# A gated linear recurrence's chunk levels, with decay products carried upward in place of per-level exponentials of log sums

## The chip, the cores and the metric

The kernel runs on one core of a Trainium2 chip. The metric is the device time of one execution in microseconds (us). Three runs of the kernel before took 2473.97, 2474.93 and 2476.08 us; their median is 2474.93 us.

## What is computed

Two layers of a decoder trunk, for 512 tokens of width 1024. Each layer normalises, projects to four token mixers (A to D) and four gates, merges the branches, and goes on with a cross-attention and a gated MLP. Only mixer C, HGRN2, is touched. Its recurrence is this, with q, log_f, k and i from the projection, four heads of 64 keys and 64 values:

```
def step(state, xs):
    qc, lfc, kc, ic = xs                       # one chunk
    b = jnp.cumsum(lfc, axis=2)
    o_inter = jnp.einsum('bhck,bhkv->bhcv', qc * jnp.exp(b), state)
    diff = b[:, :, :, None, :] - b[:, :, None, :, :]
    decay = jnp.exp(jnp.where(causal, diff, -jnp.inf))
    att = jnp.einsum('bhtk,bhtsk,bhsk->bhts', qc, decay, kc)
    o = o_inter + jnp.einsum('bhts,bhsv->bhtv', att, ic)
    b_last = b[:, :, -1:, :]
    state = (jnp.exp(b_last[:, :, 0, :])[..., None] * state
             + jnp.einsum('bhsk,bhsv->bhkv', kc * jnp.exp(b_last - b), ic))
    return state, o
```

The pair (t, s) of att needs the decay between s and t, a product over f = exp(log_f). The kernel works in chunks of 128 tokens and takes this apart by levels: at level h, blocks of 2h tokens are halved, the later half of q carries the decay from the block's middle up to t, the earlier half of k the decay from s up to the middle, and one matmul gives all pairs between the two halves. Levels h = 1, 2, 4, ..., 64, and a level 0 for the diagonal, fill the whole triangle.

## The kernel before

**Dense work.** Every projection is done as three fp32r matmuls for one (mm3, L494): high parts by high, high by low, low by high. Weights come in chunks: a DMA on SyncE, ACT's cast of the high part (whi, L483), DVE's subtraction for the low part (wlo, L484). A tile of 512 columns takes 24 such matmuls into a PSUM buffer pd.

**Order.** The class Weave (L295) interleaves dense tiles with the latency-bound chains of the branches. It keeps a modelled time of TensorE (L282); a chain that yields v comes back no sooner than about 0.86 v us of this time later, and dense work is issued meanwhile. Thus the yields in branch_c set how many dense matmuls lie between two pieces of it on TensorE. Each engine then works through its own instructions strictly in the order in which they stand.

**Around branch C.** In a layer the projection of C (Cp) comes first. Then the chain of branch C (Cb) runs between the matmuls of the projection of D (Dp) and of the gates (gb, gd, gc); the chain of branch D (Db) needs Dp and Cb; the projection of B (Bp) needs Db. Each tile of Dp leaves PSUM by DVE's L1008 (draw), then POOL subtracts the shifted tile (ddd, L1009), then DVE's L1012 makes dr, dk, dv and so on.

**branch_c.** L800 sums log_f by scans. level(h) makes one operand tile cX for a level: DVE subtracts the sum at the block's middle (L813), ACT takes the two exponentials (L814, L815), POOL multiplies one half by q (L816), the other by k (L817). Level 0 uses k and q themselves, level 1 a tile from first() (L823 to L825). The operands of a level are made one level ahead in the program. Then yield 3, and 16 matmuls (32 instructions in the trace) into four PSUM buffers of the pool ps, which has just four. Each buffer goes to the attention tile catt, by DVE under a mask (L857) or, from h = 32, by ACT (L854). Then come khat (L866 to L868), q times exp(b) (L870), the transposes of khat (L876) and the recurrence over four chunks, which ends in the tile cy (L925).

Of the kernel before, what the change touches and what calls it, by code (L numbers as in the profile page):

```python
# [13 lines left out]
AF = mybir.ActivationFunctionType  # L14
ALU = mybir.AluOpType
# [6 lines left out]
P = 128  # L22
KD = D // P
NT = S // P
# [236 lines left out]
def bc(ap, pos, n):  # L261

    shape = list(ap.shape)
    shape.insert(pos, n)
    return ap.unsqueeze(pos).to_broadcast(shape)
# [108 lines left out]
class Trunk:  # L374
    scale = 0.856
# [296 lines left out]
    def layer_consts(self, l):  # L672
# [13 lines left out]
        nc.vector.tensor_mul(t.rearrange("p (a c) -> p a c", a=2), lam[:, :, 0], lam[:, :, 1])  # L686
        nc.vector.tensor_reduce(dv[:, 8:10], t.rearrange("p (a c) -> p a c", a=2), axis=AX.X, op=ALU.add)
        nc.scalar.activation(dv[:, 8:10], dv[:, 8:10], AF.Exp)
# [101 lines left out]
    def branch_c(self, l, q, f, i, g):  # L790
        nc, ar = self.nc, self.ar
        k = ar.alloc([P, 2, 512], name='ck')
        lf = ar.alloc([P, 2, 512], name='clf')
        self.logsig(l, f, k, lf)
        yield 8
        b = f
        for j in range(2):
            for t in range(NT):
                s = slice(t * P, (t + 1) * P)
                nc.vector.tensor_tensor_scan(b[:, j, s], self.ones, lf[:, j, s], 0.0, op0=ALU.mult, op1=ALU.add)  # L800
        od = lambda x, o: x.rearrange("p j (n a) -> p j n a", a=2)[:, :, :, o]

        def flat(x):
            return x.rearrange("p j t -> p (j t)")

        def level(h):
            X = ar.alloc([P, 1024], name='cX')
            v = X.rearrange("p (n a) -> p n a", a=2 * h)
            bv = flat(b).rearrange("p (n a) -> p n a", a=2 * h)
            qv = flat(q).rearrange("p (n a) -> p n a", a=2 * h)  # L810
            kv = flat(k).rearrange("p (n a) -> p n a", a=2 * h)
            nseg = 1024 // (2 * h)
            nc.vector.tensor_sub(v, bv, bv[:, :, h - 1:h].to_broadcast([P, nseg, 2 * h]))  # L813
            nc.scalar.activation(v[:, :, h:], v[:, :, h:], AF.Exp)  # L814
            nc.scalar.activation(v[:, :, :h], v[:, :, :h], AF.Exp, scale=-1.0)  # L815
            nc.gpsimd.tensor_mul(v[:, :, h:], v[:, :, h:], qv[:, :, h:])  # L816
            nc.gpsimd.tensor_mul(v[:, :, :h], v[:, :, :h], kv[:, :, :h])  # L817
            return X.rearrange("p (j t) -> p j t", j=2), X

        def first():  # L820

            X = ar.alloc([P, 2, 512], name='cX')
            nc.scalar.activation(od(X, 1), od(lf, 1), AF.Exp)  # L823
            nc.gpsimd.tensor_mul(od(X, 1), od(X, 1), od(q, 1))
            nc.gpsimd.tensor_copy(od(X, 0), od(k, 0))  # L825
            ar.free(lf)
            return X, X


        mm = self.te.matmul  # L830
        att = [[ar.alloc([P, 4, P], name='catt') for u in range(2)] for p in range(2)]
        for a in att[0] + att[1]:
            nc.gpsimd.memset(a, 0.0)
        levels = [0, 1, 64, 32, 16, 8, 4, 2]
        nxt = ((k, q), None)
        for n, h2 in enumerate(levels):
            (lhs, rhs), Xt = nxt
            if n + 1 < len(levels):
                X, xt = level(levels[n + 1]) if n else first()
                nxt = ((X, X), xt)  # L840
            yield 3
            for u in range(2):

                ps = [self.pss().rearrange("p (n t) -> p n t", n=4) for _ in range(2)]
                for x in range(4):
                    j, o = x % 2, (2 * u + x // 2) * P
                    for p in range(2):
                        r = slice(p * 64, p * 64 + 64)
                        mm(ps[p][:, x], lhs[r, j, o:o + P], rhs[r, j, o:o + P], start=True, stop=True)
                for p in range(2):  # L850
                    a = att[p][u]
                    if h2 >= 32:
                        for c in range(0, P, 2 * h2):
                            nc.scalar.copy(a[c:c + h2, :, c + h2:c + 2 * h2],  # L854
                                           ps[p][c:c + h2, :, c + h2:c + 2 * h2])
                    else:
                        nc.vector.copy_predicated(a, bc(self.um_('U%d' % h2), 1, 4), ps[p])  # L857
            if Xt is not None:
                ar.free(Xt)

        bv = b.rearrange("p j (t a) -> p (j t) a", a=P)
        el = self.small([P, 8], 'cel', 1)
        nc.scalar.activation(el, bv[:, :, P - 1], AF.Exp)
        kh = ar.alloc([P, 2, 512], name='ckh')
        khv = kh.rearrange("p j (t a) -> p (j t) a", a=P)
        nc.vector.tensor_sub(khv, bv[:, :, P - 1:P].to_broadcast([P, 8, P]), bv)  # L866
        nc.scalar.activation(kh, kh, AF.Exp)
        nc.gpsimd.tensor_mul(kh, kh, k)  # L868
        nc.scalar.activation(b, b, AF.Exp)
        nc.vector.tensor_mul(q, q, b)  # L870
        ktm = k
        yield 6
        for j in range(2):
            ps = self.pss()
            for t in range(NT):
                self.te.transpose(ps[:, t * P:(t + 1) * P], kh[:, j, t * P:(t + 1) * P], self.c('ident'))  # L876
            nc.scalar.copy(ktm[:, j], ps)
        ar.free(kh)
        yield 2
        y = ar.alloc([P, NT, 256], name='cy')  # L880
        st = None
        for t in range(NT):
            o = t * P
            ps = self.pss()
            pv = ps[:, 0:256].rearrange("p (h v) -> p h v", h=4)
            for h in range(4):
                mm(pv[:, h], att[h % 2][t // 2][:, (t % 2) * 2 + h // 2], i[:, t, h * 64:h * 64 + 64],
                   start=h == 0, stop=t == 0 and h == 3)
            if t:
                for j in range(2):  # L890
                    mm(ps[:, j * P:(j + 1) * P], q[:, j, o:o + P], st[:, j], start=False, stop=j == 1)
            nc.scalar.copy(y[:, t], ps[:, 0:256])
            if t < NT - 1:
                p2 = self.pss()
                for h in range(4):
                    r0 = (h % 2) * 64
                    j = h // 2
                    mm(p2[r0:r0 + 64, j * 64:j * 64 + 64], ktm[:, j, o + r0:o + r0 + 64],
                       i[:, t, h * 64:h * 64 + 64], start=True, stop=True)

                new = self.cp.tile([P, 2, P], F32, tag='bd%d' % (t % 2), bufs=1, name=self.nm('cbd'))
                nc.gpsimd.memset(new, 0.0)
                for j in range(2):
                    for r0 in (0, 64):
                        r = slice(r0, r0 + 64)
                        if t == 0:
                            nc.vector.tensor_copy(new[r, j, r], p2[r, j * 64:j * 64 + 64])
                        else:
                            nc.vector.scalar_tensor_tensor(new[r, j, r], st[r, j, r],
                                                           el[r, j * 4 + t:j * 4 + t + 1],  # L910
                                                           p2[r, j * 64:j * 64 + 64], op0=ALU.mult, op1=ALU.add)
                st = new
                yield 1.5
        ar.free(att, f, i, q)
        sq = ktm
        yv = y.rearrange("p t (h v) -> p (t h) v", v=64)
        sqv = sq.rearrange("p j (n v) -> p (j n) v", v=64)
        nc.scalar.square(sqv, yv)
        ss = self.small([P, 16], 'css', 1)
        rs = self.small([P, 16], 'crs', 1)  # L920
        nc.vector.tensor_reduce(ss, sqv, axis=AX.X, op=ALU.add)
        nc.vector.tensor_scalar(ss, ss, 1.0 / 64, EPS, op0=ALU.mult, op1=ALU.add)
        self.rsqrt(rs, ss, 'r16')
        nc.gpsimd.tensor_mul(y, y, g)
        nc.vector.tensor_mul(yv, yv, bc(rs, 2, 64))  # L925
        ar.free(sq, g)
        yield 7
        out = self.to_fm(y, 2, lambda j: self.cv('hng', 0))
        ar.free(y)
        return out  # L930
# [1102 lines left out]
```

## Time and profile before

| | |
|---|---|
| median of three runs | 2474.93 us |
| the profiled execution | 2476.26 us |
| its span in the trace | 2474.5 us |
| mean granted TensorE clock | 0.990 |
| TensorE (PE) busy | 2405.6 us, 97% of the span |
| VectorE (DVE) / ScalarE (ACT) / GpSimd (POOL) busy | 62% / 40% / 20% |
| share of PE in the chain that ended last | 87% |

The busy line tells how much of the span an engine worked. The waits tell for each engine which instruction waited for which, and for how long. Windows give busy time and granted clock by stretch. The chain is the work that ended last, followed back from the end; a timeline lists one engine's instructions by start, with the idle time ahead of each and what ended it in brackets. The levels of branch C run in layer 0 at about 73 to 126 us, in layer 1 at about 1295 to 1350 us.

### The profile page before, as it was taken

Reading aid. Unit: us, or ns where it says so; the run is one execution under the profiler, and the core shown is the slowest. Engines: PE = TensorE matmul, PEld = TensorE weight load, DVE = VectorE, ACT = ScalarE, POOL = GpSimd, SP = SyncE. Lnnn points to the kernel's source line nnn. Section 1 sums busy time; section 2 is a strip of 40 time slices with the busy share of each in tenths; the row PEclk is TensorE's granted clock in tenths of the full one; section 3 lists DMA queues with packets and bytes.
Section 4 is the critical chain, followed back from the end, with each engine's and each line's share of the span. In section 5 each row is a group of like instructions: output and inputs, shape, how many; then the busy total and the mean of one; then the engine's idle time right before and its main releaser. Section 6 shows DMA issues by size and latency. Waiting matters only on the chain.

```text
span 2474.5 us, 34381 instructions
## 1 busy us (share of the span) xinstructions
PE 2405.6 (97%) x13344; PEld 2005.7 (81%) x13344; DVE 1528.1 (62%) x2731; ACT 991.9 (40%) x1759; POOL 504.7 (20%) x390
## 2 busy tenths in 40 slices
PE   8899999999999999999999999999999999999997
PEld 7777887788889888888887788877888898888886
DVE  7677356856655567367476764477566565763762
ACT  6343523444334444234362425244434354442441
POOL 2421033245010111011232200433430101110112
PEclk9999999999999999999999999999999999999998
DMA  5224334214434222222322342332243242322321
GB/s 175 84 88 157 94 115 145 73 61 146 130 106 142 77 90 98 97 99 94 133 75 71 107 150 85 120 120 73 71 160 111 98 145 68 95 93 94 102 94 60
DMA packets 89602, 259.69 MB, mean 105 GB/s; under 512 B 18144, under 2 KB 21856, under 8 KB 89440
## 3 DMA queue, kind: packets, MB, share of 16 engines
q1 hardware_dynamic: 57168, 205.81, 25.3%
q10 hardware_dynamic: 25872, 30.58, 3.8%
q0 software_dynamic: 6400, 21.11, 2.7%
q8 instruction: 105, 1.72, 0.3%
q14 instruction: 57, 0.47, 0.1%
HBM read 234.32 MB, written 23.13 MB: 104 GB/s over the span
## 4 chain that ended last, share of the span: by engine, by line
PE 87%; DVE 6%; POOL 2%; ACT 2%; issue 1%; DMA 1%; DVEq 0%; ACTq 0%; SPq 0%; POOLq 0%
PE ffn_pd L288 29%; PE A_pd L288 7%; PE Bp_pd L288 5%; PE mo_pd L288 4%; PE mq_pd L288 4%; PE mix_pd L288 4%; PE ga_pd L288 4%; PE gd_pd L288 4%; PE gc_pd L288 3%; PE Db_ps L288 3%; PE Dp_pd L288 2%; PE gb_pd L288 2%; PE mv_pd L288 2%; PE mk_pd L288 2%; PE matt_ps L288 2%; PE Cb_ps L288 2%
## 5 line engine op out<-in xcount | busy, mean ns | idle before, releaser
L483 ACT CAST whi<-wst 128x1024 fp32r<-128x1024 f32 x388 | 406.1, 1051 | 786.2 <-PE ffn_pd L288 216.1
L484 DVE TENSOR_TENSOR wlo<-wst,whi 128x1024 fp32r<-128x1024 f32 x388 | 494.4, 1278 | 213.1 <-ACT whi L483 211.9
L288 PE MATMUL ffn_pd<-xgh,whi 128*128 128x512 f32 x704 | 274.3, 390 | 0.0
L288 PE MATMUL ffn_pd<-xgh,wlo 128*128 128x512 f32 x704 | 273.9, 389 | 0.0
L288 PE MATMUL ffn_pd<-xgl,whi 128*128 128x512 f32 x704 | 273.9, 389 | 0.0
L1897 POOL TENSOR_TENSOR ffn_ft<-ffn_ft,ffn_fc 128x512 f32<-128x512 f32 x44 | 60.1, 1367 | 545.6 <-DVE ffn_fu L1883 350.3
L288 PEld LDWEIGHTS ffn_pd<-xgh,wlo 128*128 128x128 f32 x704 | 132.2, 188 | 27.7
L288 PEld LDWEIGHTS ffn_pd<-xgl,whi 128*128 128x128 f32 x704 | 132.2, 188 | 27.3
L288 PEld LDWEIGHTS ffn_pd<-xgh,whi 128*128 128x128 f32 x704 | 132.2, 188 | 27.1
L288 PE MATMUL ffn_pd<-fh,whi 128*128 128x512 f32 x352 | 136.9, 389 | 0.0
L288 PE MATMUL ffn_pd<-fl,whi 128*128 128x512 f32 x352 | 136.9, 389 | 0.0
L288 PE MATMUL ffn_pd<-fh,wlo 128*128 128x512 f32 x352 | 136.9, 389 | 0.0
L288 PE MATMUL A_pd<-xgh,whi 128*128 128x512 f32 x256 | 106.0, 414 | 0.0
L288 PE MATMUL A_pd<-xgh,wlo 128*128 128x512 f32 x256 | 101.2, 395 | 0.0
L288 PE MATMUL A_pd<-xgl,whi 128*128 128x512 f32 x256 | 100.8, 394 | 0.0
L1884 DVE TENSOR_TENSOR ffn_fu<-ffn_pd,r_rbc 128x512 f32<-128x512 f32 x88 | 60.4, 688 | 43.8 <-PE ffn_pd L288 43.6
L531 DVE TENSOR_TENSOR fl<-ffn_ft,fh 128x512 fp32r<-128x512 f32 x44 | 30.5, 693 | 90.5 <-ACT fh L530 90.5
L530 ACT CAST fh<-ffn_ft 128x512 fp32r<-128x512 f32 x44 | 27.3, 621 | 144.8 <-POOL ffn_ft L1897 144.8
L1446 POOL TENSOR_TENSOR A_rp<-A_rp,snr 128x512 f32<-128x512 f32 x24 | 50.7, 2113 | 165.4 <-DVE A_rp L1445 163.3
L575 POOL TENSOR_TENSOR mo_sqa<-mo_sqa,mo_sqt 128x512 f32<-128x512 f32 x14 | 23.6, 1685 | 297.7 <-ACT mo_sqa L571 257.7
L1886 ACT ACTIVATE ffn_fc<-ffn_fu,cvt 128x512 f32<-128x512 f32 x88 | 71.7, 817 | 26.9 <-DVE ffn_fu L1884 26.7
L288 PEld LDWEIGHTS ffn_pd<-fl,whi 128*128 128x128 f32 x352 | 66.1, 188 | 13.8
(593 smaller groups left out, 6240.6 us busy)
## 6 DMA issues: line engine op xcount, KB each, us to landing
wst<-in_wst_dram SPq DMA_DIRECT2D x388, 512.0 KB, 3.5
gb_gate<-gb_gu ACTq DMA_DIRECT2D x16, 256.0 KB, 2.2
gd_gate<-gd_gu ACTq DMA_DIRECT2D x16, 256.0 KB, 2.1
gc_gate<-gc_gu ACTq DMA_DIRECT2D x16, 256.0 KB, 2.0
pc_gu<-gc_gate POOLq DMA_DIRECT2D x16, 256.0 KB, 3.7
pd_gu<-gd_gate POOLq DMA_DIRECT2D x16, 256.0 KB, 3.2
pb_gu<-gb_gate POOLq DMA_DIRECT2D x16, 256.0 KB, 3.0
x<-in_x_dram ACTq DMA_DIRECT2D x13, 256.0 KB, 3.5
```

The costliest lines, as they stand in the source:

```text
L288: return self.te.matmul(out, lhsT, rhs, **kw)
L483: nc.scalar.copy(hi, st)
L484: nc.vector.tensor_sub(lo, st, hi.bitcast(F32))
L530: nc.scalar.copy(dst[0], src)
L531: nc.vector.tensor_sub(dst[1], src, dst[0].bitcast(F32))
L575: (eng or nc.gpsimd).tensor_add(acc[:, :n], acc[:, :n], t[:, :n])
L1446: nc.gpsimd.tensor_mul(t2, t2, self.snr)
L1884: nc.vector.tensor_mul(u[:, 2:514], ps, self.rb)
L1886: nc.scalar.activation(acc, u[:, 2:514], AF.Identity, scale=self.cv('cw2', ch), bias=self.cv('cb', ch))
L1897: nc.gpsimd.tensor_mul(th, th, cc[1])
```

## The change

The scans, level() and first() go. The decay d = exp(log_f) is taken once (by ACT, over all tokens). The levels run in the order 0, 1, 2, 4, ..., 64, and all matmuls take k and q themselves, which are changed in place between levels: after level 0, q is multiplied by f (DVE, 1024 elements a partition); after level h, the earlier half of k in each block is multiplied by the decay of the whole later half (POOL, L834) and the later half of q by that of the earlier half (DVE, L835), and d becomes the product of neighbouring pairs (L838), half as many as before. After level 64, k is khat and q is q times exp(b), and d the decay of the chunk, so the block behind the levels goes too. A level's yield is now 4.5 and stands behind it; the yield 6 ahead of the transposes has gone.

```diff
@@ -793,52 +793,23 @@
         lf = ar.alloc([P, 2, 512], name='clf')
         self.logsig(l, f, k, lf)
         yield 8
-        b = f
-        for j in range(2):
-            for t in range(NT):
-                s = slice(t * P, (t + 1) * P)
-                nc.vector.tensor_tensor_scan(b[:, j, s], self.ones, lf[:, j, s], 0.0, op0=ALU.mult, op1=ALU.add)
-        od = lambda x, o: x.rearrange("p j (n a) -> p j n a", a=2)[:, :, :, o]
-        def flat(x):
-            return x.rearrange("p j t -> p (j t)")
-        def level(h):
-            X = ar.alloc([P, 1024], name='cX')
-            v = X.rearrange("p (n a) -> p n a", a=2 * h)
-            bv = flat(b).rearrange("p (n a) -> p n a", a=2 * h)
-            qv = flat(q).rearrange("p (n a) -> p n a", a=2 * h)
-            kv = flat(k).rearrange("p (n a) -> p n a", a=2 * h)
-            nseg = 1024 // (2 * h)
-            nc.vector.tensor_sub(v, bv, bv[:, :, h - 1:h].to_broadcast([P, nseg, 2 * h]))
-            nc.scalar.activation(v[:, :, h:], v[:, :, h:], AF.Exp)
-            nc.scalar.activation(v[:, :, :h], v[:, :, :h], AF.Exp, scale=-1.0)
-            nc.gpsimd.tensor_mul(v[:, :, h:], v[:, :, h:], qv[:, :, h:])
-            nc.gpsimd.tensor_mul(v[:, :, :h], v[:, :, :h], kv[:, :, :h])
-            return X.rearrange("p (j t) -> p j t", j=2), X
-        def first():
-            X = ar.alloc([P, 2, 512], name='cX')
-            nc.scalar.activation(od(X, 1), od(lf, 1), AF.Exp)
-            nc.gpsimd.tensor_mul(od(X, 1), od(X, 1), od(q, 1))
-            nc.gpsimd.tensor_copy(od(X, 0), od(k, 0))
-            ar.free(lf)
-            return X, X
+        d = f
+        nc.scalar.activation(d, lf, AF.Exp)
+        ar.free(lf)
+        flat = lambda x: x.rearrange("p j t -> p (j t)")
+        d = flat(d)
+        dd = ar.alloc([P, 1024], name='cD')
+        nd = 0
         mm = self.te.matmul
         att = [[ar.alloc([P, 4, P], name='catt') for u in range(2)] for p in range(2)]
         for a in att[0] + att[1]:
             nc.gpsimd.memset(a, 0.0)
-        levels = [0, 1, 64, 32, 16, 8, 4, 2]
-        nxt = ((k, q), None)
-        for n, h2 in enumerate(levels):
-            (lhs, rhs), Xt = nxt
-            if n + 1 < len(levels):
-                X, xt = level(levels[n + 1]) if n else first()
-                nxt = ((X, X), xt)
-            yield 3
+        for h in (0, 1, 2, 4, 8, 16, 32, 64):
             for u in range(2):
                 ps = [self.pss().rearrange("p (n t) -> p n t", n=4) for _ in range(2)]
@@ -846,36 +817,34 @@
                     j, o = x % 2, (2 * u + x // 2) * P
                     for p in range(2):
                         r = slice(p * 64, p * 64 + 64)
-                        mm(ps[p][:, x], lhs[r, j, o:o + P], rhs[r, j, o:o + P], start=True, stop=True)
+                        mm(ps[p][:, x], k[r, j, o:o + P], q[r, j, o:o + P], start=True, stop=True)
                 for p in range(2):
                     a = att[p][u]
-                    if h2 >= 32:
-                        for c in range(0, P, 2 * h2):
-                            nc.scalar.copy(a[c:c + h2, :, c + h2:c + 2 * h2],
-                                           ps[p][c:c + h2, :, c + h2:c + 2 * h2])
+                    if h >= 32:
+                        for c in range(0, P, 2 * h):
+                            nc.scalar.copy(a[c:c + h, :, c + h:c + 2 * h], ps[p][c:c + h, :, c + h:c + 2 * h])
                     else:
-                        nc.vector.copy_predicated(a, bc(self.um_('U%d' % h2), 1, 4), ps[p])
-            if Xt is not None:
-                ar.free(Xt)
-        bv = b.rearrange("p j (t a) -> p (j t) a", a=P)
-        el = self.small([P, 8], 'cel', 1)
-        nc.scalar.activation(el, bv[:, :, P - 1], AF.Exp)
-        kh = ar.alloc([P, 2, 512], name='ckh')
-        khv = kh.rearrange("p j (t a) -> p (j t) a", a=P)
-        nc.vector.tensor_sub(khv, bv[:, :, P - 1:P].to_broadcast([P, 8, P]), bv)
-        nc.scalar.activation(kh, kh, AF.Exp)
-        nc.gpsimd.tensor_mul(kh, kh, k)
-        nc.scalar.activation(b, b, AF.Exp)
-        nc.vector.tensor_mul(q, q, b)
-        ktm = k
-        yield 6
+                        nc.vector.copy_predicated(a, bc(self.um_('U%d' % h), 1, 4), ps[p])
+            if not h:
+                nc.vector.tensor_mul(q, q, f)
+            else:
+                dv = d.rearrange("p (n a) -> p n a", a=2)
+                half = lambda x, o: flat(x).rearrange("p (n a) -> p n a", a=2 * h)[:, :, o * h:o * h + h]
+                to = lambda o: dv[:, :, o:o + 1].to_broadcast([P, 512 // h, h])
+                nc.gpsimd.tensor_tensor(half(k, 0), half(k, 0), to(1), op=ALU.mult)
+                nc.vector.tensor_tensor(half(q, 1), half(q, 1), to(0), op=ALU.mult)
+                d = dd[:, nd:nd + 512 // h]
+                nd += 512 // h
+                nc.vector.tensor_mul(d, dv[:, :, 0], dv[:, :, 1])
+            yield 4.5
+        el = d
+        ktm = ar.alloc([P, 2, 512], name='ckt')
         for j in range(2):
             ps = self.pss()
             for t in range(NT):
-                self.te.transpose(ps[:, t * P:(t + 1) * P], kh[:, j, t * P:(t + 1) * P], self.c('ident'))
+                self.te.transpose(ps[:, t * P:(t + 1) * P], k[:, j, t * P:(t + 1) * P], self.c('ident'))
             nc.scalar.copy(ktm[:, j], ps)
-        ar.free(kh)
+        ar.free(k)
         yield 2
         y = ar.alloc([P, NT, 256], name='cy')
         st = None
@@ -911,7 +880,7 @@
                                                            p2[r, j * 64:j * 64 + 64], op0=ALU.mult, op1=ALU.add)
                 st = new
                 yield 1.5
-        ar.free(att, f, i, q)
+        ar.free(att, f, i, q, dd)
         sq = ktm
         yv = y.rearrange("p t (h v) -> p (t h) v", v=64)
         sqv = sq.rearrange("p j (n v) -> p (j n) v", v=64)
```

Where instructions stand now. On POOL in layer 0, before, from the first work on branch C to the first ddd of Dp:

```order
L824 ISA
L824 TENSOR_TENSOR cX_673<-cX_673,cq_172 128x512
L825 COPY cX_673<-ck_602 128x512
L816 TENSOR_TENSOR cX_729<-cX_729,cq_172 128x8x64
L817 TENSOR_TENSOR cX_729<-cX_729,ck_602 128x8x64
...
L816 TENSOR_TENSOR cX_997<-cX_997,cq_172 128x256x2
L817 TENSOR_TENSOR cX_997<-cX_997,ck_602 128x256x2
L1009 TENSOR_TENSOR Dp_ddd_633<-Dp_draw_632 128x512
L1009 TENSOR_TENSOR Dp_ddd_690<-Dp_draw_689 128x512
```

And the same stretch of POOL in the changed kernel, where L978 is ddd and L834 the mul of k:

```order
L978 ISA
L978 TENSOR_TENSOR Dp_ddd_633<-Dp_draw_632 128x512
L978 TENSOR_TENSOR Dp_ddd_705<-Dp_draw_704 128x512
L834 TENSOR_TENSOR ck_602<-ck_602,cf_173 128x512
L978 TENSOR_TENSOR Dp_ddd_769<-Dp_draw_768 128x512
L834 TENSOR_TENSOR ck_602<-ck_602,cD_658 128x256x2
L978 TENSOR_TENSOR Dp_ddd_833<-Dp_draw_832 128x512
L834 TENSOR_TENSOR ck_602<-ck_602,cD_658 128x128x4
```

The cX operations ahead of ddd have gone, and the muls of k stand one by one between the ddd of the tiles.

On DVE in layer 0, before, the last rows ahead of the first copies into catt (L1008 is draw, L1012 the operation that needs ddd; rk and csr belong to a rotary table):

```order
L1008 TENSOR_TENSOR Dp_draw_632<-Dp_pd_592,r_rbc_291 128x512
L1007 MEMSET Dp_draw_689 128x1
L484 TENSOR_TENSOR wlo_897<-wst_894,whi_896 128x1024
L1012 SCALAR_TENSOR_TENSOR dr_587<-Dp_ddd_633,cvt_75,Dp_draw_632 128x512
L658 TENSOR_TENSOR rk_1241<-rk_1241 128x512
L659 TENSOR_SCALAR csr_1237<-rk_1241 128x512
L1008 TENSOR_TENSOR Dp_draw_689<-Dp_pd_638,r_rbc_291 128x512
L1007 MEMSET Dp_draw_786 128x1
L484 TENSOR_TENSOR wlo_964<-wst_961,whi_963 128x1024
L1012 SCALAR_TENSOR_TENSOR dr_587<-Dp_ddd_690,cvt_75,Dp_draw_689 128x512
L857 COPY_PREDICATED catt_665<-um,Cb_ps_705 128x512
L857 COPY_PREDICATED catt_667<-um,Cb_ps_706 128x512
```

In the changed kernel, DVE in layer 0 from level 4 to level 8 (L977 is draw, L981 the twin of L1012, L827 the copy, L835 the mul of q):

```order
L981 SCALAR_TENSOR_TENSOR dk_588<-Dp_ddd_833,cvt_75,Dp_draw_832 128x512
L827 COPY_PREDICATED catt_659<-um,Cb_ps_848 128x512
L827 COPY_PREDICATED catt_661<-um,Cb_ps_849 128x512
L827 COPY_PREDICATED catt_660<-um,Cb_ps_860 128x512
L827 COPY_PREDICATED catt_662<-um,Cb_ps_861 128x512
L835 TENSOR_TENSOR cq_172<-cq_172,cD_658 128x128x4
L977 TENSOR_TENSOR Dp_draw_923<-Dp_pd_838,r_rbc_291 128x512
L976 MEMSET Dp_draw_987 128x1
L484 TENSOR_TENSOR wlo_1130<-wst_1127,whi_1129 128x1024
L827 COPY_PREDICATED catt_659<-um,Cb_ps_896 128x512
L827 COPY_PREDICATED catt_661<-um,Cb_ps_897 128x512
L981 SCALAR_TENSOR_TENSOR dv_589<-Dp_ddd_924,cvt_75,Dp_draw_923 128x512
```

The subtractions of the levels have gone from DVE; each level now has its copies and then its mul of q, and the work of one tile of Dp stands around them.

On TensorE, in layer 0, before: 51 matmuls of Dp, level 0, then seven times 15 dense matmuls and a level, 27 dense ones and the transposes. Now: 36 of Dp, level 0, seven times 21 dense ones and a level, 21 and the transposes. Ahead of the matmuls of cy's transposes stand 30 matmuls of the gates in place of 38 in layer 0, 34 in place of 38 in layer 1; ahead of those of dsq in layer 0 43 in place of 46. Between the last operation of Db and Bp stand 23 in place of 43 (layer 0) and 7 in place of 24 (layer 1). From Bp on TensorE's order is the same, and no matmul is added or taken out.

## Rows read from the trace of the kernel before

**Rows 1.** The page: busy us, share of the span, instructions.

```profile
PE 2405.6 (97%) x13344; PEld 2005.7 (81%) x13344; DVE 1528.1 (62%) x2731; ACT 991.9 (40%) x1759; POOL 504.7 (20%) x390
```

**Rows 2.** Waits of PE: line, releaser: us in total, times, longest us.

```profile
PE Cb_ps L288 <- DVE catt L857: 14.5, 2, 8.8
PE Dp_pd L288 <- DVE wlo L484: 3.7, 1, 3.7
PE Db_ps L292 <- DVE dsq L1079: 3.3, 2, 2.0
...
PE Cb_ps L292 <- DVE cy L925: 2.6, 2, 2.1
```

**Rows 3.** Windows: us, busy PE PEld DVE ACT POOL, PEclk, DMA share, GB/s.

```profile
80.00:100.00 20.00, 12.32 (x89) 10.65 (x90) 15.63 (x22) 5.40 (x8) 6.93 (x5) 0.74 0.20 66
...
1280.00:1300.00 20.00, 16.29 (x84) 13.24 (x83) 20.00 (x13) 11.66 (x20) 20.00 (x11) 0.85 0.16 53
1300.00:1320.00 20.00, 14.35 (x96) 11.96 (x95) 13.36 (x19) 3.59 (x5) 8.75 (x6) 0.81 0.23 77
```

**Rows 4.** The chain of waits, layer 0: start us, us, what.

```profile
80.63 1.01 POOL Dp_ddd L1009
...
87.68 4.39 PE Cb_ps L288 x32
92.08 3.77 PE Dp_pd L288 x15
95.85 1.99 PE Cb_ps L288 x32
97.83 3.63 PE Dp_pd L288 x15
...
209.56 43.52 PE gd_pd L288 x192
```

**Rows 5.** POOL's timeline, both layers: start us, us, instruction, [idle before <- releaser].

```profile
46.95 1.73 POOL L824 TENSOR_TENSOR cX<-cX,cq 128x512 f32<-128x512 f32 x1 [15.50 <-ACT cX L823]
51.62 10.54 POOL L825 COPY cX<-ck 128x512 f32<-128x512 f32 x1 [2.93 <-ACT ck L774]
...
63.37 2.29 POOL L817 TENSOR_TENSOR cX<-cX,ck 128x512 f32<-128x512 f32 x1
...
74.00 1.26 POOL L817 TENSOR_TENSOR cX<-cX,ck 128x512 f32<-128x512 f32 x1
...
84.16 1.96 POOL L1009 TENSOR_TENSOR Dp_ddd<-Dp_draw 128x512 f32<-128x512 f32 x1 [2.53 <-DVE Dp_draw L1007]
...
97.66 2.40 POOL L868 TENSOR_TENSOR ckh<-ckh,ck 128x1024 f32<-128x1024 f32 x1
...
1274.57 0.88 POOL L825 COPY cX<-ck 128x512 f32<-128x512 f32 x1 [37.88 <-ACT ck L786]
```

**Rows 6.** DVE's timeline in the levels of layer 0.

```profile
81.66 0.75 DVE L1012 SCALAR_TENSOR_TENSOR dr<-Dp_ddd,cvt,Dp_draw 128x512 f32<-128x512 f32 x1 [11.25 <-POOL Dp_ddd L1009]
...
86.82 1.32 DVE L857 COPY_PREDICATED catt<-um,Cb_ps 128x512 f32<-128x512 uint8 x2
...
97.73 2.87 DVE L1012 SCALAR_TENSOR_TENSOR dk<-Dp_ddd,cvt,Dp_draw 128x512 f32<-128x512 f32 x1 [1.21 <-POOL Dp_ddd L1009]
...
101.66 0.68 DVE L1008 TENSOR_TENSOR Dp_draw<-Dp_pd,r_rbc 128x512 f32<-128x512 f32 x1
...
102.35 1.23 DVE L484 TENSOR_TENSOR wlo<-wst,whi 128x1024 fp32r<-128x1024 f32 x1
...
112.23 2.10 DVE L484 TENSOR_TENSOR wlo<-wst,whi 128x1024 fp32r<-128x1024 f32 x1 [0.16 <-ACT whi L483]
```

**Rows 7.** The chain of waits, layer 1.

```profile
1309.06 4.29 PE Cb_ps L288 x32
1313.35 4.06 PE Dp_pd L288 x15
```

**Rows 8.** PE's timeline, level 0 of layer 1.

```profile
1295.17 3.79 PE L288 MATMUL Cb_ps<-cq,ck 64*128 64x128 f32 x32
```

## The prediction

> **What bounds the kernel now.** The page's busy line comes first: TensorE (PE) works 97% of the span and no other engine comes near [rows 1]. An edit on another engine can then only pay where PE waits, or where the granted clock falls. The waits of PE, sorted by length, show where that is [rows 2]: the second largest entry is in the chunk levels of branch C (Cb_ps), 14.5 us in two waits, one per layer, released by the copies catt of L857. A wait of 3.7 us on wlo stands in layer 1 just ahead of its second one. The windows give the other half of the loss [rows 3]: the granted clock is 0.74, 0.85 and 0.81 of full speed in the 20 us around these waits.
>
> Two things are behind the wait. The chain shows POOL muls of L816 and L817 one behind the other until 80.63 us in layer 0, and only then L1009 (ddd), which DVE waits for, and behind DVE's L1012 the copies [rows 4]. The POOL timeline says why it is late: it has a copy and 13 muls to do in one row, each 1.26 us alone and up to 2.29 us, and the copy took 10.54 us [rows 5]. DVE works in order, so L1012 stood idle 11.25 us for ddd with the catt copies queued behind it [rows 6]. A level fills all four ps buffers, so the next level cannot begin before they are copied: PE waited 8.8 us. Layer 1 has the same row on POOL without the slow copy (0.88 us there), and its wait is 5.7 us (14.5 less 8.8).
>
> **What the loss is worth.** A level takes 1.99 us at full clock and the 15 dense matmuls between two levels 3.63 us [rows 4]. After the wait the level took 4.39 us, about twice: the granted clock was at 1.2 instead of 2.4 GHz. Layer 0 loses 8.8 + (4.39 - 1.99 = 2.4) + (3.77 - 3.63 = 0.1) = 11.3 us. Layer 1 loses 5.7 + 3.7 of waits, 3.79 - 1.99 = 1.8 on its level 0, 4.29 - 1.99 = 2.3 on the level after, 4.06 - 3.63 = 0.4 on the block after that [rows 7, 8], and 0.8 on the block that ran between (1309.06 less the 5.7 of wait less 1298.96, where level 0 ended, is 4.4 against 3.63), in all 14.7 us. Together **26.0 us**, about 1% of the time, and that is all there is to gain here unless other stages move.
>
> **The change part by part.** *What goes:* the log sums (scan, 6 subtractions), the exponentials per level and 14 of POOL's cX operations; khat's subtraction, exponential and mul. All this is off PE, and its worth is the 26.0 us if nothing new is late. In the new order POOL's first work is ddd, and DVE's L1012 twin no longer waits behind a row of muls. So the catt waits go. In layer 1 DVE and POOL are both busy in all of the 20 us ahead of the wait [rows 3], on the subtractions and muls, with wlo queued among them; these go too, so its 3.7 us goes.
>
> *What comes per level:* PE has the same 16 matmuls per branch level, and now 21 dense ones between levels instead of 15. A dense matmul is 43.52 / 192 = 0.227 us [rows 4]; 15 of them are 3.40 and the block took 3.63, so a switch adds 0.23. A block of 21 is 4.77 + 0.23 = 5.0, the period 1.99 + 5.0 = 7.0 us. DVE must do in a period: 7/8 of a dense tile (21 of 24 matmuls) and the level's own work. A tile costs it 0.68 (draw), 1.23 (wlo), 0.75 (L1012) and, where wlo lies beside ddd, 2.10 - 1.23 = 0.87 more [rows 6], 3.53 together, 7/8 of it 3.1. The level's own is four copies at 1.32 / 2 = 0.66, 2.64, and the half mul of q; as a 128x512 operation it is bounded by draw and L1012, I take 0.69. Sum **6.4 of 7.0 us**. DVE keeps up, with little to spare. The products d are tiny tiles and lie behind the q mul; they go with it.
>
> *Where it is tight:* the new order puts, at levels 4 and 8, a tile's end right at the level's start. From the level's start: draw to 0.7, ddd (1.01 to 1.96 [rows 4, 5]) to 2.7 at most, L1012's twin to 3.4, four copies to 6.1, q mul to 6.8, against a next level due at 7.0. In layer 1 another small DVE operation (dkk) stands in this row and uses the slack up. Also, POOL's k mul starts right behind ddd, so beside L1012's twin. The trace has this once: L1012 took 2.87 instead of 0.75 us beside the POOL mul L868 of 2.40 us [rows 5, 6]. The k mul is half as wide and takes 1.26 us, so I charge 1.3 less the slack. Low bound: no wait at all, 0. High bound: all four tight levels wait 1.3 and layer 1 half a us more for dkk, 4 x 1.3 + 2 x 0.5 = 6.2, with up to one clock fall of 2.4 in each layer, 11. The small waits that the trace shows (cy 2.1, dsq 2.0 [rows 2]) are the nearest; I take 1.5 us per layer, **3.0 us**.
>
> *The k mul on POOL:* 1.26 us (2.29 contended) from the level's end at 2.0 or ddd's at 2.7, done by 5.0 at the latest, due at 7.0. Costed at nothing; the cover is the block of 21 dense matmuls. If the cover were 15, 5.0 would still be inside 5.6.
>
> Whether DVE's copies suffer beside the k mul is the other open price. The trace has wlo, both inputs in SBUF, at 2.10 beside ddd and at 1.23 without; of a copy out of PSUM beside a POOL mul it has no clean case. The Trainium skill (GPSIMD Engine Reference, section 1, Specifications) has VectorE and GpSimd share SBUF interfaces, with contention for DVE instructions that have two SBUF inputs. By that rule, wlo, L1012 and the q mul suffer, the catt copies with one input in PSUM don't; the wlo rows agree as far as they go.
>
> *What moves behind the levels:* the transposes, cy, Db and gates shift against the dense work on PE: ahead of the transposes of Cb stand 21 matmuls instead of 27, ahead of cy's 30 instead of 38 in layer 0 and 34 instead of 38 in layer 1; after the last operation of Db, 23 instead of 43 and 7 instead of 24. From Bp on PE's order is the same. The waits there now are 2.6 (cy) and 3.3 us (dsq) in both layers [rows 2]. khat needs no work ahead of the transposes any more. Ahead of cy 4 to 8 matmuls less are 0.9 to 1.8 us more wait where there is one; dsq has 43 instead of 46 ahead in layer 0. Bounds -2 and +3; I take 0, since the earlier start of the whole chain offsets it.
>
> **Sum.** 26.0 - 3.0 = 23.0 us. The profiled execution took 2476.3 us (span 2474.5), 1.3 above the median of the runs, so 2476.3 - 23.0 = 2453.3 there and 2474.9 - 23.0 = **2452** for the median. With the bounds: waits 0 and cy -2 give 2447, waits of 11 and cy +3 give 2463; I narrow it to 2446 to 2458 for this case, since both ends need all terms to go one way.
>
> **Rivals.** *First: POOL's first mul pays a one-off.* The copy of 10.54 us in layer 0 against 0.88 in layer 1 [rows 5] is 9.7 us for something that occurs once. If it is a cost of POOL's first operations, it lands on the first ddd; some 4 us of it are covered, then PE waits 5.3 and the level after runs at half clock, 2.4: 2452 + 7.7 = 2460. Against it: the first mul L824 came ahead of the copy and took 1.73, and the new kernel has no POOL copy there. The Trainium skill (GPSIMD Engine Reference, section 2.1, Instruction dispatch) says that the first call of a freshly loaded kernel pays a load of about 6 us; by that figure the wait would be 1.6 us, 2452 + 1.6 + 2.4 = 2456, an estimate. The rows put it on another operation. 7%.
>
> *Second: DVE is the bound of each level.* If the copies too are slowed beside the k mul, by its 1.3 us in 6.4, DVE needs 7.7 of 7.0 us and PE waits 0.7 in each of five levels with DVE copies behind a k mul, plus the tight ones' 3: 5 x 0.7 x 2 layers = 7, 2452 + 7 = 2459. For it: 2.10 against 1.23 for wlo. Against: the copies' input in PSUM. 8%.
>
> *Third, slower:* the levels are now a serial chain. Before, the operands cX of all levels could be made ahead; now each level's k and q wait for the last matmul of the one before, and the next level for the mul. If the k mul with its broadcast operand takes far longer than a plain one, each of 14 gaps (7 per layer) waits. A wait of 1.5 us with the level at half clock costs 1.5 + 2.4 = 3.9, 14 times 55: 2475 - 26 + 55 = 2504. It decides from 26 / 14 = 1.9 us per gap, that is a k mul of over 7.0 + 1.9 - 2.7 = 6.2 us (4.3 before anything waits), with the clock kept; POOL's muls with strided operands in the trace are at 1.26 to 2.29 [rows 5]. 5%.
>
> *Fourth: no change.* The wait only moves, for instance to cy and Db, whose cover is thinner; 20 us would have to come back in stages with 6 us of waits now. 2475. 5%.
>
> **How the numbers follow.** The forecast has 75%. A run of this kernel tells a change from none from about 0.2%, 5 us. Faster: 75 + 7 + 8 = 90%; same 5%; slower 5%. The range from 2444 to 2461 leaves out the third and fourth rival and about 4% at each end of the first cases.
>
> **What would show it.** Right: no PE wait on the catt copies over 2 us, granted clock 1.00 in the levels of both layers, ddd the first POOL mul with about 1 to 2 us, L834 at 1.3 to 2.3, the copies still at 0.66, and waits of PE under 1.5 us at levels 8 and 16. Wrong: a first POOL operation of many us (first rival), copies near 1.3 (second), L834 over 4 us (third), waits on cy, dsq or Bp that have grown by 10 us or more (fourth).

## The result, and the profile after

The changed kernel takes 2490.11 us (median of 4 runs, 2486.84 to 2490.42) against 2474.45 us before (4 runs too): a ratio of 1.0059 with a 95% interval of 1.0042 to 1.0077. It is 0.6% **slower**; 2452 us, faster, was forecast, with a range that ended at 2461. The profiled execution took 2490.42 us, its span is 2488.6 us. One run among all that follow, of e5, took 10464 us in place of 2454 to 2455 and is left out.

The surprise is that what was forecast for the waits and the clock of the levels came true. These are the waits of PE after (line, releaser: us in total, times, longest):

```profile
PE Bb_ps L292 <- DVE bp L1497: 14.5, 13, 1.9
PE Cp_pd L288 <- ACT xgh L533: 9.8, 1, 9.8
PE Db_ps L292 <- DVE dsq L1048: 4.9, 2, 2.6
...
PE Cb_ps L292 <- DVE cy L894: 2.1, 2, 1.4
...
PE Cb_ps L288 <- DVE cq L835: 0.6, 1, 0.6
```

The 14.5 us on catt and the 3.7 us on wlo [rows 2] have gone; what the levels wait for now is 0.6 us for q. The windows of the stretches around the levels (us, busy PE, PEld, DVE, ACT, POOL, then the granted clock, DMA share, GB/s) have the clock at full speed, where it was at 0.74 and 0.81 [rows 3]:

```profile
80.00:100.00 20.00, 20.00 (x141) 16.03 (x143) 17.13 (x25) 4.55 (x5) 6.14 (x6) 1.00 0.23 77
...
1300.00:1320.00 20.00, 20.00 (x155) 16.19 (x155) 17.71 (x24) 3.15 (x3) 6.63 (x5) 1.00 0.17 54
```

So the time was lost elsewhere, and PE's busy time says what kind of loss it is. The page's busy line after:

```profile
PE 2439.0 (98%) x13344; PEld 1996.5 (80%) x13344; DVE 1513.4 (61%) x2729; ACT 973.4 (39%) x1728; POOL 455.6 (18%) x374
```

PE has the same 13344 instructions and is busy 33 us longer than in [rows 1], although less of them ran at half clock. The chain shows where. These are long pieces of undisturbed dense work and, of after, also a level and the block of 21 behind it (start us, us, what), first before, then after:

```profile
754.82 23.03 PE mk_pd L288 x192
...
884.53 348.19 PE ffn_pd L288 x1536
```

```profile
99.15 2.06 PE Cb_ps L288 x32
101.20 5.10 PE Dp_pd L288 x21
...
661.80 44.80 PE mix_pd L288 x192
...
753.18 22.72 PE mk_pd L288 x192
...
883.25 358.39 PE ffn_pd L288 x1536
```

1536 matmuls of the MLP, hundreds of us behind the change and with nothing to wait for, take 358.39 us in place of 348.19: 0.2333 us each against 0.2267, at a granted clock of 1.00 in both. The blocks of 256 columns that are shown (mk) became a little faster, 22.72 against 23.03. It is so in all of the dense work: from the start of one matmul of 512 columns to that of the next, the mean over some 7,700 steps is 0.2273 us before and 0.2331 us after, some 45 us in all, of which 1,890 steps of 256 columns (0.1204 and 0.1179 us) give 5 back. The two MLPs alone cost 20 us.

TensorE's instructions and their order there are the same in both kernels. What differs for them is where the tiles lie. The built programs place the pools one behind the other in each partition of SBUF: constants, weight buffers, small tiles, arena. The change takes out one small tile, cel (8 numbers, 32 bytes), and all of the arena moves down by 32 bytes:

```
first byte of               before    after
the weight buffers           33952    33952
the arena (activations)     113824   113792
difference, modulo 256           0      224
```

The experiments ask whether these 32 bytes are the cause.

### The profile page after: what moved, and what is told of

The parts are those of the page before. It is cut to its first block, busy times and chain, and to the rows that moved or that the text cites. A ratio compares the mean times of both kernels' runs of the same rounds, so it can differ in the third digit from the quotient of the medians.

```text
span 2488.6 us, 34307 instructions
## 1 busy us (share of the span) xinstructions
PE 2439.0 (98%) x13344; PEld 1996.5 (80%) x13344; DVE 1513.4 (61%) x2729; ACT 973.4 (39%) x1728; POOL 455.6 (18%) x374
## 3 DMA queue, kind: packets, MB, share of 16 engines
q8 instruction: 105, 1.72, 0.3%
## 4 chain that ended last, share of the span: by engine, by line
PE 92%; DVE 5%; ACT 1%; issue 1%; DMA 1%; POOL 0%; DVEq 0%; ACTq 0%; SPq 0%
PE ffn_pd L288 30%; PE A_pd L288 7%; PE Bp_pd L288 5%; PE gc_pd L288 4%; PE Cp_pd L288 4%; PE gd_pd L288 4%; PE mq_pd L288 4%; PE mo_pd L288 4%; PE mix_pd L288 4%; PE ga_pd L288 4%; PE Dp_pd L288 3%; PE Db_ps L288 3%; PE gb_pd L288 2%; PE matt_ps L288 2%; PE mk_pd L288 2%; PE mv_pd L288 2%
## 5 line engine op out<-in xcount | busy, mean ns | idle before, releaser
L288 PEld LDWEIGHTS ffn_pd<-fh,wlo 128*128 128x128 f32 x352 | 66.1, 188 | 16.1
```

Source lines behind the costliest of these rows:

```text
L288: return self.te.matmul(out, lhsT, rhs, **kw)
```

## The experiments

Theory P: dense matmuls are slower because the streamed activations now lie otherwise against the weights. Theory N: the new work or its order does it. Theory T: TensorE pauses less and therefore runs slower.

**e1, the tile back.** In branch_c of the changed kernel:

```diff
+        self.small([P, 8], 'pad', 1)
```

> The changed kernel with one unused tile of 32 bytes a partition put back into the pool of small tiles, where the small tile cel stood before. It moves the arena (all large tiles, so the activations that the dense matmuls stream) back by 32 bytes, to where it lay in the kernel before; instructions and their order stay. Theory P (placement): the dense 512-column matmul takes 0.2333 us in the changed kernel and 0.2267 before because the change took 32 bytes out ahead of the arena. Then a block of 192 goes back from 44.80 to 43.5 us and the time to 2452 us or a little under (2444 to 2456). Theory N (new program): the slowness comes with the new work or its order itself, and the time stays at 2490, a block of 192 at 44.8. Theory T (TensorE pauses less in the levels and so runs slower elsewhere): stays at 2490 too.

Measured: 2450.1 us, 0.990 of before (0.9884 to 0.9917). The same two blocks in its chain:

```profile
743.80 23.03 PE mk_pd L288 x192
873.48 348.22 PE ffn_pd L288 x1536
```

40 us come back by 32 unused bytes, with every instruction as it was. N and T fall. This kernel is also faster than both.

**e2, the same 32 bytes in the kernel before.**

```diff
+        self.small([P, 8], 'pad', 1)
```

> The kernel before with one unused tile of 32 bytes more among the small tiles, so that its arena starts a multiple of 64 bytes, as in the changed kernel, in place of 32 beyond one. Nothing else is changed. Theory P: a block of 192 dense matmuls takes 44.8 us in place of 43.5 and the time is 2515 us (2505 to 2525): 2474 and the some 40 us by which the changed kernel missed 2450. Theories N and T: 2474, as the program and its pauses are those of before.

Measured: 2517.1 us, 1.0169 (1.0153 to 1.0184), the MLP's block at 358.39. The old kernel becomes slower by 41 us with no change in its work.

**e3 and e4, the weights moved.** An unused tile among the constants moves the weights by 32 bytes; e4 has that and e1's.

```diff
+        self.cp.tile([P, 8], F32, name='pad')
```

> The changed kernel with an unused tile of 32 bytes among the constants, ahead of the weight buffers and the arena. Weights then start at a multiple of 64 bytes (they lay 32 beyond one in both kernels), the arena 32 beyond one, as before. If the place of the streamed activations alone decides: 2452 us, a block of 192 at 43.5. If it matters that weights and arena lie at a different offset: 2490, a block at 44.8, as they differ here and in the changed kernel, and agree in the kernel before. N and T: 2490.

> The changed kernel with both unused tiles, so that weights and arena start at multiples of 64 bytes. If the place of the streamed activations alone decides: 2490 us, a block of 192 at 44.8. If it matters that they differ: 2452, a block at 43.5, since they agree here. N and T: 2490.

Measured: e3 2489.5 us with the block at 358.39, e4 2449.4 us with 348.23. With these, e1 and e2, two places of the weights (33952 and 33984) have met the same two places of the arena (113824 and 113856): a difference of 0 modulo 256 is fast, 32 more or less slow, and neither place alone decides.

**e5, e10, e11, e13, e14: other differences.** The pad of e1 was made larger, to 24 numbers in e5, and to 40, 264, 72 and 136 in e10, e11, e13 and e14. Each differs from e1 by nothing but the arena's place (and that of the small tiles behind the pad).

```diff
-        self.small([P, 8], 'pad', 1)
+        self.small([P, 24], 'pad', 1)
```

> The changed kernel with an unused tile of 96 bytes among the small tiles in place of 32. Weights lie 32 beyond a multiple of 64 and of 128 bytes as ever; the arena now lies 32 beyond a multiple of 64, but 96 beyond one of 128. If the two have to agree to 64 bytes: a block of 192 dense matmuls at 43.5 us and 2450 us as with 32 bytes. If they have to agree to 128 bytes: 44.8 and 2490.

> The changed kernel with an unused tile of 160 bytes: arena and weights lie at the same offset to 128 bytes, as in the kernel before, but differ by 128 to 256. With 96 bytes (agreement to 64, not to 128) a block of 1536 dense 512-column matmuls took 351.6 us against 348.2 and one of 192 256-column matmuls 21.8 against 23.0. If agreement to 128 bytes is all that counts: 348.2 and 23.0, 2450 us. If a coarser distance counts too: other values, between 345 and 358 and between 21.5 and 23, and a time between 2445 and 2490.

> The changed kernel with an unused tile of 1056 bytes: arena and weights agree to 1024 bytes and differ by 1024 to 2048, while in the kernel before they agree to 2048. If agreement to 128 bytes is all that counts: as with 32 bytes, a block of 1536 at 348.2 us, one of 192 256-column matmuls at 23.0, 2450 us. If a coarser distance counts: other values there, and a time between 2445 and 2490.

> The changed kernel with an unused tile of 288 bytes: arena and weights agree to 256 bytes and differ by 256 to 512. By the runs so far a difference of 0 and of 1024 costs nothing (348.2 us for a block of 1536), 64 a third (351.6), 32, 96 and 128 all (358.4). If only small differences collide: 348.2 and 2450 us. If everything but a multiple of some larger distance costs: 351 to 359 and 2455 to 2490.

> The same with 544 bytes, a difference of 512 to 1024. As with 288: 348.2 and 2450 us if only small differences collide or 512 is a multiple of the distance that counts, 351 to 359 and 2455 to 2490 if not.

Measured, in the order of the difference of arena and weights modulo 2048 bytes:

| kernel | difference | 1536 matmuls, 512 columns | 192 matmuls, 256 columns | time |
|---|---|---|---|---|
| e1 | 0 | 348.2 us | 23.03 us | 2450.1 us |
| e2 (the work of before) | 32 | 358.4 us | 22.40 us | 2517.1 us |
| e5 | 64 | 351.6 us | 21.76 us | 2454.8 us |
| e10 | 128 | 358.4 us | 22.78 us | 2489.0 us |
| e13 | 256 | 348.2 us | 23.03 us | 2450.4 us |
| e14 | 512 | 348.2 us | 23.03 us | 2450.1 us |
| e11 | 1024 | 348.2 us | 23.03 us | 2450.2 us |
| after | 32 less than 0 | 358.4 us | 22.72 us | 2490.1 us |

Among the differences tried, multiples of 256 bytes are all alike and best for 512 columns. In e10 the difference is 128, so agreement to 128 bytes is not enough, which was one of the two answers named. Whether the other differences also repeat every 256 bytes was not tried. The 256-column blocks of mk want another difference (64 is best of those tried), but there are fewer matmuls of 256 columns than of 512: 1,920 against 8,176.

**e12, only the low weights.** A pad between the buffers of the high and of the low weights moves the latter by 32 bytes and, with them, the arena back to where it was.

```diff
+            if n == 0:
+                self.wp.tile([P, 8], F32, name='pad')
             lo = self.wp.tile([P, 1024], F32R, tag='wlo', bufs=self.wb[2], name='wlo%d' % n)
```

> The changed kernel with an unused tile of 32 bytes between the buffers of the high weights and those of the low ones. Arena and high weights then agree as in the kernel before; only the low weights lie 32 bytes off. Of three dense matmuls one takes low weights. If the cost arises for each pair of streamed activations and the weights they meet (or the weights that load meanwhile): one matmul of three at 0.233 us and two at 0.227, a block of 1536 at 351.6 us, and 2463 us. If one tile off its place slows everything: 358 and 2490. If low weights do not matter: 348.2 and 2450.

Measured: 2490.8 us, the block at 358.38; by the totals, one tile off its place cost as much as all. The starts in PE's timeline say more. Three rows of e12 (xgh and fh are high activations, xgl and fl low ones; start us, us):

```profile
999.78 0.39 PE L288 MATMUL ffn_pd<-fh,wlo 128*128 128x512 f32 x1
1000.01 0.40 PE L288 MATMUL ffn_pd<-fh,whi 128*128 128x512 f32 x1
1000.25 0.40 PE L288 MATMUL ffn_pd<-fl,whi 128*128 128x512 f32 x1
```

Rows printed to 0.01 us are too coarse for single steps, and a mean over them does not help: three matmuls take 0.680 us in e1 and 0.700 us in e12, whole hundredths, so each step is rounded the same way every time. These are means of the starts in nanoseconds that the traces hold, over some 1,050 steps of each kind in the two MLPs:

| from the start of | to that of | e1 | e12 | after |
|---|---|---|---|---|
| xgh, whi | xgl, whi | 226.5 ns | 232.3 ns | 233.3 ns |
| xgl, whi | xgh, wlo | 226.7 ns | 239.2 ns | 233.5 ns |
| xgh, wlo | the next xgh, whi | 227.0 ns | 228.4 ns | 233.2 ns |

All three steps became longer in e12, by 5.8, 12.5 and 1.4 ns. The most falls to the step into the matmul with the low weights, which had moved, but the step between two matmuls with high weights, which had not, grew as well. So the cost is not confined to the pairs that touch the moved tile. Of the answers named, the first (a third of the cost) was wrong, and what came is the second: one tile off its place slows the whole row as much as all of them off it.

**e6, ddd on DVE in the kernel before.** Now the prediction's own theory of the waits.

```diff
-                nc.gpsimd.tensor_sub(dd, raw[:, 0:512], raw[:, 1:513])
+                nc.vector.tensor_sub(dd, raw[:, 0:512], raw[:, 1:513])
```

> The kernel before, with ddd (L1009) done by DVE in place of POOL, so that it no longer stands behind POOL's row of cX muls; TensorE's order and all places in SBUF stay. Theory of the prediction (DVE idles for ddd behind that row, with the catt copies behind it): the 8.8 us wait of layer 0 and its clock loss of 2.5 go, and of layer 1 the 5.7 us and the 2.7 after it; the wlo wait of 3.7 there with the 2.6 on level 0 and the block behind it may stay, since the muls and subtractions still lie beside each other. 2475.7 - 20 = 2456 us (2450 to 2463). Rival (the levels wait for the cX operands or for DVE's own work, and ddd only comes last by the profile): 2474 to 2476, the wait on catt stays over 5 us.

Measured: 2470.1 us, 0.9978 (0.9968 to 0.9987): 6 us gained, not 20. Neither theory holds as a whole. The wait on catt fell from 14.5 to 9.2 us, and DVE's timeline shows what is left of it:

```profile
69.61 2.32 DVE L484 TENSOR_TENSOR wlo<-wst,whi 128x1024 fp32r<-128x1024 f32 x1
71.85 1.78 DVE L1012 SCALAR_TENSOR_TENSOR dr<-Dp_ddd,cvt,Dp_draw 128x512 f32<-128x512 f32 x1
73.56 1.74 DVE L658 TENSOR_TENSOR rk<-rk 128x512 f32<-128x512 f32 x1
...
75.33 1.38 DVE L659 TENSOR_SCALAR csr<-rk 128x512 f32<-128x512 f32 x1
...
77.35 1.05 DVE L1009 TENSOR_TENSOR Dp_ddd<-Dp_draw 128x512 f32<-128x512 f32 x1
78.33 2.28 DVE L484 TENSOR_TENSOR wlo<-wst,whi 128x1024 fp32r<-128x1024 f32 x1
80.53 1.97 DVE L1012 SCALAR_TENSOR_TENSOR dr<-Dp_ddd,cvt,Dp_draw 128x512 f32<-128x512 f32 x1
82.42 2.55 DVE L857 COPY_PREDICATED catt<-um,Cb_ps 128x512 f32<-128x512 uint8 x4
```

DVE no longer idles, but beside POOL's muls wlo takes 2.28 us in place of 1.23 and L1012 1.97 in place of 0.75 [rows 6], L658 1.74 in place of 0.69 and L659 1.38 in place of 0.43 (the rows of before at 82.33 and 83.05 us). The copies start at 82.4 us, 4.4 earlier than before, where 8.8 would have been needed. The edit has a part in that: the ddd of two tiles, some 2.1 us, are now DVE's own work ahead of the copies. The six slowed operations come to 6.4 us, the larger part.

**e9, without the muls.** L816 and L817 are left out of the kernel before, so q and k are missing in levels 2 to 64.

```diff
-            nc.gpsimd.tensor_mul(v[:, :, h:], v[:, :, h:], qv[:, :, h:])
-            nc.gpsimd.tensor_mul(v[:, :, :h], v[:, :, :h], kv[:, :, :h])
```

> The kernel before without the 12 POOL muls per layer of L816 and L817 (q and k are left out of levels 2 to 64; their matmuls run on the exponentials alone). ddd is on POOL again, with nothing long ahead of it, and DVE has nothing on POOL beside it; subtractions, exponentials and TensorE's work stay. Theory (the row of muls makes both waits, half as a queue ahead of ddd, half by slowing DVE beside it, which is why ddd on DVE alone gave back 6 us): the waits on catt and wlo fall from 18 us to under 2, the clock stays at 1.00 in both layers' levels, 2476 - 25 = 2451 us (2447 to 2455). Rival (DVE is late by its own subtractions and wlo): a wait on catt of 3 us or more stays in each layer, 2460 to 2468 us.

Measured: 2448.6 us, 0.9895 (0.988 to 0.991), with no wait on catt or wlo at all, and these windows:

```profile
80.00:100.00 20.00, 20.00 (x175) 16.54 (x172) 14.87 (x19) 8.49 (x17) 5.30 (x3) 1.00 0.16 53
1280.00:1300.00 20.00, 19.77 (x157) 15.86 (x154) 16.13 (x22) 6.83 (x14) 7.36 (x4) 1.00 0.23 79
```

The row of muls made both waits and the fall of the clock, about 27 us, partly as a queue ahead of ddd and partly by slowing DVE; how much each would cost alone no run separates. Subtractions and exponentials, still in, make no wait in the levels.

**e7, 15 matmuls between levels.** e1 with the levels' yield as before:

```diff
-            yield 4.5
+            yield 3
```

> The changed kernel with the 32 bytes put back and the levels' yield at 3 in place of 4.5, so 15 dense matmuls between levels again in place of 21. Theory of the prediction (DVE's row of a period decides, 6.4 us of 7.0 with 21): with 15, DVE has 2.2 for 15/24 of a tile and 3.3 of the level's own, 5.5 us of 5.6, and where a tile ends at the level's start draw, ddd, L981, copies and q mul take 6.8 against 5.6. PE waits about 1 us in four or five levels of each layer, 8 to 10 us, and more if the clock falls behind a wait: 2460 us (2455 to 2475). Rival (the spacing does not matter, as copies and muls of two levels run side by side): 2450 us, waits on cq or catt under 2 us in all.

Measured: 2460.4 us, with these waits of PE:

```profile
PE Cb_ps L288 <- DVE cq L836: 6.1, 5, 2.0
PE Cb_ps L292 <- DVE cy L895: 6.0, 2, 5.0
```

Five waits for q, 6.1 us, and cy 6.0 us instead of 2.4 in e1. The spacing matters, as DVE's row of a period said. The total came out as forecast (10 us), in part by luck, since a third of it lies behind the levels, where nothing was charged.

**e8, the mul of k on DVE.** e1 with one engine changed:

```diff
-                nc.gpsimd.tensor_tensor(half(k, 0), half(k, 0), to(1), op=ALU.mult)
+                nc.vector.tensor_tensor(half(k, 0), half(k, 0), to(1), op=ALU.mult)
```

> The changed kernel with the 32 bytes put back and the mul of k (L834) on DVE in place of POOL. It adds 0.7 us to DVE's 6.4 in a period of 7.0. Theory of the prediction (DVE has 0.6 us to spare per level): PE waits 0.1 us in all levels and about 0.7 more at the tight levels 4 and 8, so 2 to 5 us: 2453 us (2450 to 2456). Rival (DVE is far from its bound, since L981 no longer lies beside a POOL mul): 2450 us, no new wait over 0.5 us.

Measured: 2452.4 us (2450.48 to 2453.74) against e1's 2450.1 (2448.23 to 2453.1); the ranges overlap, so the times tell little. Three waits for q, 0.9 us in all, none over 0.5, against one of 0.7 us in e1: DVE has more to spare than the sum of 6.4 of 7.0 us made it.

## Why the prediction was wrong

**The loss that the change removes: right.** 26.0 us were read from the rows, and 23.0 forecast after the new waits. e1, the change at the old placement, gains 25.6 us over its runs of before, new waits included, and e9 27.2. At 2450.1 us, e1 lies inside the range of the forecast.

**What the waits were made of: half right.** That L1012 stood idle 11.25 us for ddd is the last link of the chain, and I took the queue on POOL for all of it. e6 shows that slowing DVE beside POOL is the other half: with the queue out of the way it still holds the copies back. Since the change takes out the muls, both halves go, and that the sum came out right was luck in this respect.

**The new waits: on the high side.** I charged 3.0 us; the trace of e1 has 0.7 us for q, and of the levels' neighbours, charged at nothing, dsq rose from 3.3 to 5.2 us and cy fell from 2.6 to 2.4. The mechanism is there: ahead of the only wait, a twin of L1012 took 1.64 us in place of 0.75, and the chain of e1 in layer 1 runs over just the operations that the prediction put in a row (start us, us, what):

```profile
1297.98 1.99 POOL Dp_ddd L979
...
1299.99 1.64 DVE dk L982
1301.63 1.26 DVE catt L828 x2
1302.89 0.36 DVE dkk L1037
1303.26 1.26 DVE catt L828 x2
1304.52 0.58 DVE cq L836
...
1305.23 2.06 PE Cb_ps L288 x32
1307.29 4.98 PE Dp_pd L288 x21
```

It happened once instead of four times, because ddd mostly took 1.04 us and the twin mostly stood free of the mul. The period is 7.04 us here; 7.0 was worked out.

**The rivals.** None occurred. The first ddd took 1.04 us, and the muls of k 1.08 to 1.70 in layer 0, from POOL's timeline after:

```profile
68.84 1.04 POOL L978 TENSOR_TENSOR Dp_ddd<-Dp_draw 128x512 f32<-128x512 f32 x1 [36.18 <-DVE Dp_draw L976]
...
94.23 1.16 POOL L834 TENSOR_TENSOR ck<-ck,cD 128x512 f32<-128x512 f32 x1 [1.02 <-PE Cb_ps L288]
...
101.36 1.70 POOL L834 TENSOR_TENSOR ck<-ck,cD 128x512 f32<-128x512 f32 x1 [0.36 <-PE Cb_ps L288]
108.47 1.08 POOL L834 TENSOR_TENSOR ck<-ck,cD 128x512 f32<-128x512 f32 x1 [5.42 <-PE Cb_ps L288]
```

The copies of catt did not suffer beside them, but L1012's twin did. Two rows of DVE in layer 0, the first beside the k mul of 94.23 us:

```profile
94.22 1.72 DVE L981 SCALAR_TENSOR_TENSOR dk<-Dp_ddd,cvt,Dp_draw 128x512 f32<-128x512 f32 x1
95.86 2.57 DVE L827 COPY_PREDICATED catt<-um,Cb_ps 128x512 f32<-128x512 uint8 x4
```

1.72 us beside the mul against 0.75 without. In layer 0, two copies ran beside the mul at 101.36 us, 102.00 to 103.34, and took 1.34 us, as two take alone [rows 6]. The Trainium skill (GPSIMD Engine Reference, section 1, Specifications) names DVE instructions with two SBUF inputs, or in a 2-port perf mode, as those that contend with GpSimd; the rows of the twin and of the copies agree. Two inputs are not needed, though. dkk has one tensor input, and in e1 its first row lies beside the k mul of 1292.67 us, its second beside none:

```profile
1292.77 1.49 DVE L1037 TENSOR_SCALAR dkk<-dk,cvt 128x512 f32<-128x512 f32 x1
...
1302.78 0.47 DVE L1037 TENSOR_SCALAR dkk<-dk,cvt 128x512 f32<-128x512 f32 x1
```

The prediction's price of dkk, half a us, left this out. Whether dkk runs in such a perf mode no run shows.

**The step that failed** is the price of a dense matmul, which the sum took as fixed. The prediction rests on "An edit on another engine can then only pay where PE waits, or where the granted clock falls" and says, of what moves behind the levels, "From Bp on PE's order is the same." I took the same order at the same clock for the same time, and all dense matmuls at the 0.227 us of the old trace. The block of 21 in the levels was put at 5.0 us; it took 4.99 in e1 and 5.10 in the changed kernel, 2% more, and the MLP's block 3% more. No term of the sum and no rival had a change of this price, though the edit that causes it, el = d in place of the small tile cel, stands in the diff, and the places of all tiles stand in the built program. With some 8,000 such matmuls, it outweighs everything else that the change does: 40 us lost by the place of the arena (after against e1) against 25.6 gained.

**What stays open.** Why a difference of 128 bytes is as bad as one of 32 and 256 costs nothing was not found; the runs show only that the difference between the places of the streamed tiles and of the weights decides it, and that three matmuls take 0.680 us at 0 and 0.700 us at 32, 128 and 32 less than 0. Why the three steps of e12 share the cost so unequally is open too. Differences of 96, 160 and 192 bytes were not tried. That the POOL copy L825 takes 10.5 us in layer 0 was not settled either: in e9, with no muls behind it, it still took 10.54.

## What to carry to other kernels

When tiles are added or taken out, compare the addresses of the operands that TensorE streams and of the weights it loads, before and after: here 32 bytes of a small tile that no dense matmul reads were worth 1.6% of the time, and an unused pad that makes the difference a multiple of 256 bytes again gave it back. A first sign in a profile is a block of identical matmuls, with nothing to wait for and at full clock, that has another length per matmul. And where a chain of waits ends at a queue on one engine, look whether the engine that waits for it is also slowed by that queue before giving the queue the whole wait.

## What the runs showed of the hardware

Two things were not expected. The step from one dense 128x512 matmul to the next depends on the byte offset between the streamed tile and the weights: 0.2267 us on average at a difference of 0, 256, 512 or 1024 bytes, 0.2289 at 64, 0.2333 at 32, at 128 and at 32 less than 0. For the 256 columns of mk the order is another: 0.1200 us at 0, 0.1186 at 128, 0.1183 at 32 less than 0, 0.1167 at 32, 0.1133 at 64. And beside a POOL mul not only DVE's operations with two tensor inputs are slowed but also ones with one: dkk took 1.49 us in place of 0.47, L659 1.38 in place of 0.43, while copies out of PSUM kept their time.
